# The up projection of a ConvFFN on fp16 halves, with a scale measured by squares in the mLSTM, and the next unit's first products inside a unit

## The chip, the cores and the metric

The kernel runs on one core of one Trainium2 chip. The metric is device time in microseconds (us), the median of several runs. The engines are PE (matrix), DVE (vector), ACT (scalar functions), POOL and SP; each works through a queue of its own in order, and a DMA is started by a row in one of these queues. PEld is PE's loading of weights.

## The reference

One layer of a diffusion backbone: 1024 latent tokens of width 1024, and 256 context tokens. Both are normalised, modulated and projected; windowed attention and a bidirectional chunkwise mLSTM (4 heads, chunks of 128, so 2 context and 8 latent chunks in each direction) work side by side; the branches are gated and merged, and a ConvFFN with 2816 hidden channels follows. What the change touches is the FFN's up projection, and the mLSTM beside which its scale is now measured:

```python
def conv_ffn(h, w_up, conv_w, conv_b, w_down):      # h (1,1024,1024), w_up (1024, 5632)
    u = h @ w_up
    up = jnp.pad(u, ((0, 0), (1, 1), (0, 0)))
    acc = conv_b
    for j in range(3):
        acc = acc + up[:, j:j + L] * conv_w[j]
    a, g = jnp.split(acc, 2, axis=-1)
    return (jax.nn.silu(g) * a) @ w_down

# in the layer
ht, ht_c = mlstm_bidirectional(...)                 # scans over chunks, state C, n, m
ml = mlstm_readout(ht, mo, ml_norm_w[l])            # rms_norm(h) * norm_w * sigmoid(mo)
y = merge_branches(att, ml, ga, gm, w_branch_att[l], w_branch_ml[l], w_out[l])
x_mid = x + g1[:, None, :] * y
x = x_mid + g2[:, None, :] * conv_ffn(modulate(rms_norm(x_mid, norm2_w[l]), sh2, sc2), w_up[l], ...)
```

## The kernel before

Products that need more than one half-precision pass are made of pairs: an operand is split into a high part and a low part, and high x high, high x low and low x high are summed in PSUM (the three matmul lines 163 to 165 and, in `product`, 2027 to 2029). `split_from` makes a pair: ACT copies to the high part (L47), DVE subtracts it from the source for the low part, with one tensor_tensor (L54) where there is no scale and one scalar_tensor_tensor (L56) where a scale is given. The combined input projection has fp16 pairs with a scale measured from the weights; the up projection and the branch products have fp32r pairs without a scale.

The up projection runs in 22 units (`NFC`, 128 hidden channels and their 128 gates each). A unit multiplies 1024 x 256 weight columns by the 1024 tokens with seven products in place of eight (a Winograd scheme of 2 x 2 blocks): two first products with `b11` and `b21` on the raw left columns (`r1`), then `t2`, `t1` (on `q1`), `t3`, `b22` (on `q2`) and `t4` (on `r2`). Each is 4 blocks of 3 matmuls 128x128 by 128x512. `Units.lead` loads a unit's weights (1 MB) and splits `r1`; `prep` and `prep2` form the sums `s` on DVE and split `q1`, `q2` and `r2`. `rest` runs the five later products; PSUM banks `pa` and `pb` are used two and three times in a unit and are emptied to the outputs `ua` and `ug` between. Behind a unit, `conv_gate` applies the width-3 convolution, the SiLU and the gate (L2165 to L2171), and `weight_sums` and `hidden_sums` make sums for the down projection (L1906, L2182 to L2185). After the units the down projection follows (`dx`, L2027 again), and there `last_row` (L2306, L2308) forms the second half of a modulation vector row by row on DVE.

In the mLSTM each head has `proj_kv` (k and v for 8 latent chunks, L47 copies k and VH out of PSUM), `proj_q`, `masked`, `states`, `core` (the recurrence: state C on DVE, its high part CH on ACT, outputs nm out of PSUM on ACT, L1487), `proj_o` (output gate mo), `readout` (squares of the result hf on ACT, a power on POOL, L1520 and L1521, and the scaling of hf on DVE, L1524) and `turn` (transposes mt on PE, L1532, and the gated product mo on DVE, L1534). The next head's projections are written between; after the last head the branch products follow (yb, with operands baa and baw).

The order of the work on each engine is set by the framework's scheduler, by its own estimates of when work is ready, and not by the order in which the program is written; tiles come from pools with a fixed number of buffers, and a new tile waits until an old one's readers are done.

Of the kernel before, what the change touches and what calls it, by code (L numbers as in the profile page):

```python
# [18 lines left out]
P = 128  # L19
# [153 lines left out]
def layer_kernel(ctx: ExitStack, tc: tile.TileContext, A: dict, out: bass.AP, dbg=None):  # L173
# [69 lines left out]
    E.hs = cp.tile([P, 2], F32, name="hs")  # L243
    E.w2 = ScaledWeights(E, tc, ph1)
# [1017 lines left out]
def stage_mlstm(E, st):  # L1262
# [84 lines left out]
    def proj_q(h):  # L1347
# [4 lines left out]
        for t in range(2):  # L1352
# [3 lines left out]
            split_from(nc, qh, ql, ps, scale=f[:, 4:5])  # L1356
            qT.append((qh, ql))
# [16 lines left out]
    def proj_o(h):  # L1374
        w = H[h]["wqo"]
        sgs = [rp.tile([P, 2, 512], F32, tag="sg", name=f"sg{h}_{t}", bufs=2) for t in range(2)]
        for t in halves(h):
            for v in range(2):
# [3 lines left out]
                nc.scalar.activation(sgs[t][:, v], ps, fn, scale=H[h]["fqo"][:, 4:5])  # L1382
        H[h]["sg"] = sgs
# [182 lines left out]

    rwp = st.enter_context(tc.tile_pool(name="mlr4", bufs=4, reuse_waits="tile"))
# [7 lines left out]
    E.kvx.close()  # L1575
    trans_k(0)
# [3 lines left out]
    for _ in range(2):  # L1580
        branch_sums()
    for h in range(MLH):
# [14 lines left out]
        if h + 1 < MLH:  # L1597
            proj_q(h + 1)
            for _ in range((3, 4, 3)[h]):
                branch_sums()  # L1600


def stage_tail(E, st):
# [51 lines left out]


# [179 lines left out]
    def norm_factors():  # L1836

        nc.vector.scalar_tensor_tensor(m2[:, 1], m2[:, 1], 1.0, vecT[:, V_N2 : V_N2 + KT], op0=ALU.add, op1=ALU.mult)
        nc.vector.tensor_scalar(m2[:, 1], m2[:, 1], float(D) ** 0.5, None, op0=ALU.mult)

# [43 lines left out]
    def put(m, k, src, s=slice(0, 512)):  # L1884
        if B.setdefault(m, [None] * H)[k] is None:
            B[m][k] = [x512(f"{m}{x}{k}", pool=homes[m]) for x in "hl"]
# [50 lines left out]
    def weight_sums(k, a0, a1, b0, b1, eng=None):  # L1937
# [11 lines left out]
        nc, lambda j: A["w_up"][j], lambda n: rawp.tile([P, KT, 256], F32, tag="raw", name=n), op4, op2,  # L1949
# [14 lines left out]
    norm_factors()  # L1964
# [19 lines left out]
    U.prep_apart(0, lambda n, dt=F32R: x512(n, dt, 1))  # L1984
# [47 lines left out]
class Units:  # L2032
# [3 lines left out]
    def __init__(self, nc, src, raw, op4, op2, bank, out, B):  # L2036
        self.nc, self.src, self.raw, self.op4, self.op2, self.bank, self.out, self.B = nc, src, raw, op4, op2, bank, out, B
# [10 lines left out]
    def pair(self, j, nm, new, src):  # L2048
        p = self.v(new(f"{nm}h{j}")), self.v(new(f"{nm}l{j}"))
        split_from(self.nc, *p, src)  # L2050
        return [(p[0][:, k], p[1][:, k]) for k in range(p[0].shape[1])]

    def lead(self, j):
        self.raws[j] = raw = self.raw(f"ur{j}")
        self.nc.sync.dma_start(raw, self.src(j))
        if j != 2:
            self.R1[j] = self.pair(j, "r1", self.op4, raw[:, :, 0:P])

    def lead_first(self, j):
# [3 lines left out]
        self.R1[j] = self.pair(j, "r1", self.op4, raw)  # L2063
# [20 lines left out]
    def prep(self, j):  # L2084
# [6 lines left out]
        self.Q[j] = [self.pair(j, "q1", self.op4, s12)]  # L2091

    def prep2(self, j):
# [5 lines left out]
        self.Q[j] += [self.pair(j, "q2", self.op4, s34), self.pair(j, "r2", self.op2, a22)]  # L2099

    def prep_apart(self, j, new):
# [3 lines left out]
        s1, s2, s3, s4 = [self.v(new(f"s{i}_{j}", F32)) for i in range(1, 5)]  # L2105
# [4 lines left out]
        self.Q[j] = [sum([self.pair(j, f"q1{i}", new, s) for i, s in enumerate((s1, s2))], [])]  # L2110
        self.S[j] = s3, s4

    def prep2_apart(self, j):
        h, lo = [self.v(self.op4(f"q2{x}{j}")) for x in "hl"]
        for i, s in enumerate(self.S.pop(j)):
            split_from(self.nc, h[:, 4 * i : 4 * i + 4], lo[:, 4 * i : 4 * i + 4], s)
        r2 = self.pair(j, "r2", self.op2, self.raws.pop(j)[:, 4:8, P:256])
        self.Q[j] += [[(h[:, k], lo[:, k]) for k in range(8)], r2]

    def rest(self, j):  # L2120
        nc, B, op = self.nc, self.B, self.op
        pa, ua = self.mid.pop(j)
        if j not in self.Q:
            self.prep(j)
        if len(self.Q[j]) == 1:
            self.prep2(j)
# [17 lines left out]
def stage_ffn(E, st):  # L2144
# [94 lines left out]
    a = None  # L2239
    for j in range(NFC):  # L2240
        if j > 2:
# [207 lines left out]
```

## Time and profile before

| | us |
|---|---|
| median of 3 runs (1845.82 to 1847.97) | 1846.55 |
| the profiled execution | 1849.14 |
| its span | 1847.4 |
| PE busy | 1790.8 (97%) |
| DVE busy | 1425.9 (77%) |
| ACT busy | 1069.8 (58%) |
| POOL busy | 508.3 (28%) |
| mean granted TensorE clock | 0.988 of full speed |

The span starts with the projection and attention; the mLSTM's own work lies at about 600 to 955, the branch products and the merge to about 1200, the up projection from there to about 1640, and the down projection to the end. Rows of the profile read: line, engine, operation, output <- input, and count; then busy time and mean time of one, and idle time of the engine before it with what ended it. A time at a row's start is from the span's start.

### The profile page before, as it was taken

What the parts mean: (1) busy time and instruction counts of PE and PEld (TensorE: products, weight loads), DVE (VectorE), ACT (ScalarE), POOL (GpSimd) and SP (SyncE); (2) the same over time, 40 slices, a digit from 0 to 9 for tenths busy, and PEclk for the clock granted to TensorE, in tenths of its full rate; (3) what the DMA queues carried; (4) which work ended last, traced back from release to release, by engine and by line L of the source; (5) the groups of instructions that cost most, each with busy time, mean ns of one, the idle gap of its engine ahead of it and who ended that gap; (6) DMA issues with size and microseconds to landing.
All of it is one profiled execution on the core that took longest, in us unless ns stands there. A gap on an engine that the chain in (4) does not pass through costs nothing.

```text
span 1847.4 us, 27864 instructions
## 1 busy us (share of the span) xinstructions
PE 1790.8 (97%) x9207; PEld 1283.5 (69%) x9207; DVE 1425.9 (77%) x2864; ACT 1069.8 (58%) x2229; POOL 508.3 (28%) x747
## 2 busy tenths in 40 slices
PE   7989999999998899999999999999999999999999
PEld 3855555555554566656668887878888888888887
DVE  3858888888788686858687787698889898897665
ACT  4747877878787565645356462476444444465441
POOL 2467769587862530303010020000000000000000
PEclk9999999999999899999999999999999999999999
DMA  9747988888796625261359927322454544599751
GB/s 342 233 138 146 201 170 179 192 180 199 147 182 131 219 79 192 79 213 37 132 188 368 344 92 246 141 77 106 172 207 180 194 160 166 195 318 371 260 172 69
DMA packets 302193, 342.47 MB, mean 185 GB/s; under 512 B 176208, under 2 KB 200672, under 8 KB 299232
## 3 DMA queue, kind: packets, MB, share of 16 engines
q1 hardware_dynamic: 287648, 314.47, 56.3%
q10 hardware_dynamic: 14400, 26.22, 4.2%
q8 instruction: 72, 1.18, 0.3%
q14 instruction: 73, 0.60, 0.1%
HBM read 224.61 MB, written 76.16 MB: 163 GB/s over the span
## 4 chain that ended last, share of the span: by engine, by line
PE 78%; DVE 7%; DMA 4%; issue 3%; ACT 3%; POOL 3%; SPq 0%; ACTq 0%; DVEq 0%; POOLq 0%
PE g L706 8%; PE pq L706 6%; PE pa L2027 4%; PE pa L2029 4%; PE pa L2028 4%; PE po L706 3%; PE dx L2029 2%; PE dx L2027 2%; PE dx L2028 2%; PE pb L2027 2%; PE pb L2029 2%; PE pb L2028 2%; PE yb L2029 2%; PE yb L2027 2%; PE yb L2028 2%
## 5 line engine op out<-in xcount | busy, mean ns | idle before, releaser
L850 DVE CUSTOM_DVE_ANT_0 s<-s,maskA,nsink 128x640 f32<-128x640 f32 (+1 forms) x128 | 117.4, 917 | 65.5 <-PE s L845 65.0
L866 DVE TENSOR_TENSOR P<-s,P 128x640 f16<-128x640 f32 (+1 forms) x128 | 100.6, 786 | 1.0 <-ACT s L861 1.0
L860 ACT ACTIVATE P<-s,st 128x640 f16<-128x640 f32 (+1 forms) x128 | 98.2, 767 | 4.1
L706 PE MATMUL g<-hH,fh 128*128 128x512 f16 x256 | 97.1, 379 | 0.0
L706 PE MATMUL g<-hH,fl 128*128 128x512 f16 x256 | 97.0, 379 | 0.0
L706 PE MATMUL g<-hL,fh 128*128 128x512 f16 x256 | 97.0, 379 | 0.0
L861 ACT ACTIVATE s<-s,st 128x640 f32<-128x640 f32 (+1 forms) x128 | 93.8, 733 | 0.0
L706 PEld LDWEIGHTS <-hH 128*128 128x128 f16 x640 | 62.8, 99 | 37.3 <-issue 1.8
L858 ACT ACTIVATE st<-st,shift 128x1 f32<-128x1 f32 x128 | 37.6, 294 | 85.6 <-DVE st L850 84.8
L706 PE MATMUL pq<-wha,hH 128*128 128x384 f16 (+1 forms) x256 | 84.9, 332 | 0.1
L706 PE MATMUL pq<-wha,hL 128*128 128x384 f16 (+1 forms) x256 | 84.9, 332 | 0.0
L706 PE MATMUL pq<-wla,hH 128*128 128x384 f16 (+1 forms) x256 | 84.9, 332 | 0.0
L706 PEld LDWEIGHTS <-fh 128*128 128x128 f16 x512 | 49.2, 100 | 45.4
L2165 ACT ACTIVATE cv<-ua,vecT 128x1024 f32<-128x1024 f32 x22 | 27.4, 1246 | 84.9 <-DVE ua L2138 84.9
L1436 POOL TENSOR_SCALAR kwh<-k,gcall 128x128 fp32r<-128x128 f32 x72 | 32.5, 455 | 157.2 <-PE dC L164 53.9
L47 ACT ACTIVATE dfh<-drf 128x512 fp32r<-128x512 f32 x55 | 34.4, 628 | 59.3 <-PE dx L2028 26.5
L2027 PE MATMUL dx<-dwh,dfh 128*128 128x512 f32 (+1 forms) x176 | 68.3, 388 | 0.0
L2029 PE MATMUL dx<-dwh,dfl 128*128 128x512 f32 (+1 forms) x176 | 68.2, 388 | 0.0
L2028 PE MATMUL dx<-dwl,dfh 128*128 128x512 f32 (+1 forms) x176 | 68.2, 387 | 0.0
L54 DVE TENSOR_TENSOR dfl<-drf,dfh 128x512 fp32r<-128x512 f32 x55 | 37.6, 688 | 36.1 <-ACT dfh L47 36.1
L165 PE MATMUL kv<-whkv,hL 128*128 128x384 f16 x192 | 62.6, 326 | 0.0
L164 PE MATMUL kv<-wlkv,hH 128*128 128x384 f16 x192 | 62.6, 326 | 0.0
(691 smaller groups left out, 6249.9 us busy)
## 6 DMA issues: line engine op xcount, KB each, us to landing
ur<-in_w_up SPq DMA_DIRECT2D x22, 1024.0 KB
wmb<-in_w_modB SPq DMA_DIRECT2D x48, 256.0 KB
f_d<-cv SPq DMA_DIRECT2D x22, 512.0 KB
wm<-in_w_modA SPq DMA_DIRECT2D x16, 512.0 KB
fr<-in_w_g SPq DMA_DIRECT2D x32, 256.0 KB
drf<-fs_d SPq DMA_DIRECT2D x15, 512.0 KB
drw<-wt_d SPq DMA_DIRECT2D x14, 512.0 KB
w1b<-in_w_cx SPq DMA_DIRECT2D x16, 388.0 KB
```

The lines of the kernel that those rows point to most:

```text
L54: rest = nc.vector.tensor_tensor(lo, src, whole, op=ALU.subtract)
L164: nc.tensor.matmul(ps, lh[:, ls], rl[:, rs], start=False, stop=False)
L165: nc.tensor.matmul(ps, ll[:, ls], rh[:, rs], start=False, stop=stop and i == n - 1)
L706: nc.tensor.matmul(self.ps, x, w, start=self.i == 0, stop=self.i == self.n - 1)
L850: nc.vector.tensor_tensor_reduce(e, e, self.mask, scale=self.ss[:, h : h + 1], scalar=nsink[:, hh : hh + 1], op0=ALU.add, op1=ALU.min, acc ...
L858: nc.scalar.activation(m, st4[:, 8 + h : 9 + h], AF.Identity, bias=shift)
L860: nc.scalar.activation(two[:, :W], e, AF.Exp, bias=m, scale=-1.0)
L861: nc.scalar.activation(e, e, AF.Exp, bias=m, scale=-1.0, accum_out=st4[:, 4 + h : 5 + h])
L866: nc.vector.tensor_tensor(two[:, W : 2 * W], self.e[h], two[:, :W], op=ALU.subtract)
L2027: nc.tensor.matmul(ps, lh, rh, start=start and i == 0, stop=False, skip_group_check=True)
L2028: nc.tensor.matmul(ps, lh, rl, start=False, stop=False, skip_group_check=True)
L2029: nc.tensor.matmul(ps, ll, rh, start=False, stop=stop and i == n - 1, skip_group_check=True)
```

## The change

Three things are changed.

1. The up projection's operands are fp16 pairs. The two halves of a pair share one tile, so a pair takes half the bytes. The weights' splits are given a scale, `E.upf[:, 2:3]`, and so use L56 in place of L54; the token operands (`b11`, `t1` and so on) are split without one.
2. The scale is measured: the up weights (23 MB) are loaded once more in 44 pieces of 512 KB from ACT's queue, 3 buffers in all, and squared with a running sum by 44 ACT instructions of 128x1024. These are written into heads 1 to 3's `proj_kv` and `proj_q` and heads 0 to 2's `proj_o`. `up_scales`, behind the last head's `proj_o`, sums them over partitions with a ones-matmul and makes the factors on DVE and POOL; it also scales the modulation `m2` and the convolution's columns.
3. In a unit from the third on, the next unit's two first products stand inside: t2, t1, next b11, t3, b22, next b21, t4. The next unit's `prep` and `prep2` are written between these, and `lead` two units ahead.

```diff
+    def up_load():
+        n = UP["load"]
+        if n < NUP:
+            raw = UP["raw"][n] = upp.tile([P, 4, 256], F32, tag="up", name=f"um{n}")
+            nc.scalar.dma_start(raw, A["w_up"][n // 2][:, 4 * (n % 2) : 4 * (n % 2) + 4])
+            UP["load"] += 1
+    def up_square(k):
+        for _ in range(k):
+            ...
+                nc.scalar.activation(raw, raw, AF.Square, accum_out=E.up[:, n : n + 1])
+                UP["done"] += 1
+                up_load()
+    def up_scales():
+        f, g, m2, vecT = E.upf, E.upf[:, 8:], E.m2[:, 1:3], E.vecT
+        ...
+        nc.tensor.matmul(pb[:, : NUP + 2], E.ones, E.up[:, : NUP + 2], start=True, stop=True)
+        nc.vector.tensor_reduce(f[:, 0:1], pb[:, :NUP], axis=AX.X, op=ALU.add)
+        nc.vector.tensor_scalar(g[:, 2:4], pb[:, NUP : NUP + 2], 1.0, 1e-30, op0=ALU.mult, op1=ALU.add)
+        nc.gpsimd.tensor_scalar(f[:, 1:2], f[:, 0:1], 2.0 ** -28, 1e-36, op0=ALU.mult, op1=ALU.add)
+        nc.gpsimd.tensor_tensor(f[:, 2:3], f[:, 1:2], expo[:, 0:1], op=ALU.pow)
+        ...
+        nc.gpsimd.tensor_tensor(f[:, 3:4], g[:, 4:5], expo[:, 0:1], op=ALU.pow)
+        nc.vector.reciprocal(f[:, 4:6], f[:, 2:4])
+        nc.gpsimd.tensor_tensor(f[:, 6:7], f[:, 4:5], f[:, 5:6], op=ALU.mult)
+        nc.gpsimd.tensor_scalar(m2, m2, f[:, 3:4], None, op0=ALU.mult)
+        cw = vecT[:, V_CW : V_CW + 132]
+        nc.gpsimd.tensor_scalar(cw, cw, f[:, 6:7], None, op0=ALU.mult)
...
 proj_kv, for h > 0 and each latent chunk:
+            if h and j >= NCB:
+                up_square(1)
 proj_q, for h > 0 and each half:
+                up_square(2 if h == MLH - 1 else 1)
 proj_o, each product:
+                if h < MLH - 1:
+                    up_square(1)
+        if h == MLH - 1:
+            up_scales()
...
     def pair(self, j, nm, new, src):
-        p = self.v(new(f"{nm}h{j}")), self.v(new(f"{nm}l{j}"))
-        split_from(self.nc, *p, src)
+        p = [self.v(t) for t in new(f"{nm}{j}")]
+        split_from(self.nc, *p, src, scale=self.scale)
...
     def rest(self, j, new=None, between=lambda i: None):
         ...
         product(nc, pb, op(q1, 0), B["t1"], True)
         copy_act(nc, ug[:, t1], pb)
+        between(0)
+        if new is not None:
+            r1 = self.R1.pop(new)
+            na, un = self.bank("A", f"pa{new}"), self.out("u", f"ua{new}")
+            product(nc, na, self.op(r1, 0), B["b11"], True)
+            copy_act(nc, un[:, t0], na)
         product(nc, pa, op(q2, 0), B["t3"], False)
         nc.vector.tensor_tensor(ug[:, t1], pa, ug[:, t1], op=ALU.add)
+        between(1)
         product(nc, pb, op(q2, 4), B["b22"], False)
         nc.vector.tensor_tensor(ua[:, t1], pb, ua[:, t1], op=ALU.add)
+        if new is not None:
+            pc = self.bank("C", f"pc{new}")
+            product(nc, pc, self.op(r1, 4), B["b21"], True)
+            nc.vector.tensor_tensor(un[:, t0], pc, un[:, t0], op=ALU.add)
+            self.mid[new] = na, un
         product(nc, pa, op(r2, 0), B["t4"], False)
```

At the end of the mLSTM, DVE's queue held the two groups of hf one behind the other (the number at a name's end tells tiles apart, `rr_0` and `rr_1` are the two halves' factors):

```order
L1524 TENSOR_SCALAR hf_11521<-hf_11521,rr_0_12050 128x256 x4
L1524 TENSOR_SCALAR hf_11521<-hf_11521,rr_1_12065 128x256 x4
L1534 SCALAR_TENSOR_TENSOR mo_0_0_12085<-mt_0_0_12080,mlw,sg_0_11944 128x512
L1534 SCALAR_TENSOR_TENSOR mo_0_1_12093<-mt_0_1_12088,mlw,sg_0_11944 128x512
L54 TENSOR_TENSOR bawl_0_12182<-bawr_12179,bawh_0_12181 128x512
L54 TENSOR_TENSOR baal_0_12228<-baar_12225,baah_0_12227 128x512
L54 TENSOR_TENSOR bawl_1_12184<-bawr_12179,bawh_1_12183 128x512
```

Now, in the same place of DVE's queue:

```order
L1533 TENSOR_SCALAR hf_11658<-hf_11658,rr_0_12207 128x256 x4
L1606 TENSOR_REDUCE upf<-upq 128x1
L1607 TENSOR_SCALAR upf<-upq 128x2
L1533 TENSOR_SCALAR hf_11658<-hf_11658,rr_1_12222 128x256 x2
L1615 RECIPROCAL upf<-upf 128x2
L1533 TENSOR_SCALAR hf_11658<-hf_11658,rr_1_12222 128x256 x2
L1543 SCALAR_TENSOR_TENSOR mo_0_0_12242<-mt_0_0_12237,mlw,sg_0_12081 128x512
L1543 SCALAR_TENSOR_TENSOR mo_0_1_12250<-mt_0_1_12245,mlw,sg_0_12081 128x512
```

The reduction, which reads the ones-matmul's result `upq`, stands between the groups, and the reciprocal between the halves of the second. On POOL, at the same place, the two halves' factors were followed by nothing of the mLSTM; now the queue reads (with what each waits for):

```order
L1529 TENSOR_SCALAR rr_1_12222<-rr_1_12222 128x4 [waits Activation_49]
L1608 TENSOR_SCALAR upf<-upf 128x1 [waits DVE_49]
L1530 TENSOR_TENSOR rr_1_12222<-rr_1_12222,expo 128x4 [waits Pool_49]
L1609 TENSOR_TENSOR upf<-upf,expo 128x1 [waits Pool_49]
L1610 TENSOR_TENSOR upf<-upf,expo 128x1 [waits DVE_49]
L1611 TENSOR_TENSOR upf<-upf 128x1 [waits Pool_49]
L1612 TENSOR_SCALAR upf<-upf 128x1 [waits Pool_49]
L1613 TENSOR_SCALAR upf<-upf 128x1 [waits Pool_49]
L1614 TENSOR_TENSOR upf<-upf,expo 128x1 [waits Pool_49]
```

The second half's power (L1530) stands behind a step that waits for DVE's reduction. Inside the mLSTM, ACT's queue in the second head's `proj_kv` held, before, copies of k and VH and squares of the next head's weights (wjw):

```order
L47 ACTIVATE k_8_8638<-kv_8_8639,wfw_ml_8492 128x128
L47 ACTIVATE VH_8_8665<-kv_8_8639,wfw_ml_8492 128x256
L1550 DMA s_ba_1_9024<-in_w_ba 128x512 x2
L112 ACTIVATE wjw_ml_1_9684,wqw_ml_9681<-wrw_ml_1_9675 128x768
L112 ACTIVATE wjw_ml_2_9686,wqw_ml_9681<-wrw_ml_2_9677 128x768
```

Now, between copies of the same kind, it holds squares of the up weights (um) and the loads of later pieces:

```order
L47 ACTIVATE k_8_8664<-kv_8_8665,wfw_ml_8515 128x128
L47 ACTIVATE VH_8_8691<-kv_8_8665,wfw_ml_8515 128x256
L1592 ACTIVATE um_8698,upq<-um_8698 128x1024
L1592 ACTIVATE um_8734,upq<-um_8734 128x1024
L1584 DMA um_8822<-in_w_up 128x1024
L47 ACTIVATE k_7_8700<-kv_7_8701,wfw_ml_8515 128x128
L47 ACTIVATE VH_7_8727<-kv_7_8701,wfw_ml_8515 128x256
```

The squares of the next head's weights stand later in the queue. In the up projection, DVE's queue held, before, from the next unit's sum with `pc` to its next sum (units 9 to 11):

```order
L1906 TENSOR_TENSOR wb_16066<-wb_16066 128x512
L2167 SCALAR_TENSOR_TENSOR cv_31_16083<-ug_15975,vecT,cv_31_16083 128x1023
L2077 TENSOR_TENSOR ua_16116<-pc_16091,ua_16116 128x512
L54 TENSOR_TENSOR q1l_16196<-s_11_16192,q1h_16195 128x1024
L2171 TENSOR_TENSOR cv_9_16079<-cv_9_16079,cv_31_16083 128x1024
L2097 TENSOR_TENSOR s_11_16199<-ur_16186 128x512
L2098 TENSOR_TENSOR s_11_16199<-ur_16186,s_11_16192 128x512
L54 TENSOR_TENSOR r2l_16207<-ur_16186,r2h_16206 128x512
L54 TENSOR_TENSOR q2l_16203<-s_11_16199,q2h_16202 128x1024
L54 TENSOR_TENSOR r1l_16334<-ur_16331,r1h_16333 128x1024
L2136 TENSOR_TENSOR ug_16120<-pa_16090,ug_16120 128x512
```

Now (from unit 12's last sum, with the preparations of units 15 to 17):

```order
L2208 TENSOR_TENSOR ua_16383<-pb_16489,ua_16383 128x512
L2259 TENSOR_TENSOR fa_16605<-fa_16605 128x512
L2164 TENSOR_TENSOR s_15_16823<-ur_16736 128x512
L2260 TENSOR_TENSOR fs_16606<-cv_11_16478,fa_16605 128x512
L2241 SCALAR_TENSOR_TENSOR cv_12_16614<-ua_16383,vecT,cv_12_16614 128x1023
L2212 TENSOR_TENSOR ua_16524<-pc_16573,ua_16524 128x512
L2242 SCALAR_TENSOR_TENSOR cv_12_16614<-ua_16383,vecT,cv_12_16614 128x1023
L2165 TENSOR_TENSOR s_15_16823<-ur_16736,s_15_16789 128x512
L56 SCALAR_TENSOR_TENSOR r_16965<-ur_16872,upf,r_16965 128x512
L2241 SCALAR_TENSOR_TENSOR cv_34_16618<-ug_16490,vecT,cv_34_16618 128x1023
L56 SCALAR_TENSOR_TENSOR q_16826<-s_15_16823,upf,q_16826 128x1024
L2242 SCALAR_TENSOR_TENSOR cv_34_16618<-ug_16490,vecT,cv_34_16618 128x1023
```

The next unit's sum with its second first product (`pc`) comes right behind the unit's own last sum, the splits are L56, and the preparations run up to three units ahead of the products, where they ran one to two ahead. The eight rows of `last_row` for the first piece (`u<-w_modB`) stood behind all units and now stand among the sums of units 2 to 8.

More of the change, by code (lines that the diff above doesn't have):

```diff
@@ L1581, in stage_mlstm @@
         branch_sums()
+    for _ in range(3):
+        up_load()
     for h in range(MLH):
@@ L1600, in stage_mlstm @@
                 branch_sums()
+    ux.close()
 def stage_tail(E, st):
@@ L2032, with __init__ @@
 class Units:
-    def __init__(self, nc, src, raw, op4, op2, bank, out, B):
-        self.nc, self.src, self.raw, self.op4, self.op2, self.bank, self.out, self.B = nc, src, raw, op4, op2, bank, out, B
+    def __init__(self, nc, src, raw, op4, pair4, pair2, scale, bank, out, B):
+        self.nc, self.src, self.raw, self.op4, self.pair4, self.pair2, self.bank, self.out, self.B = nc, src, raw, op4, pair4, pair2, bank, out, B
+        self.scale = scale
         self.raws, self.R1, self.mid, self.S, self.Q = {}, {}, {}, {}, {}
```

92 lines of the change are left out of this document (60 added, 32 removed).

## The prediction

> **What bounds the kernel now.** I read the page's busy times and chain first, to see which engine can be the limit; then the windows by stage, since the average mixes stages; then the matmuls of two stages one by one, for the price of each type.
>
> ```profile
> PE 1790.8 (97%) x9207; PEld 1283.5 (69%) x9207; DVE 1425.9 (77%) x2864; ACT 1069.8 (58%) x2229; POOL 508.3 (28%) x747
> PE 78%; DVE 7%; DMA 4%; issue 3%; ACT 3%; POOL 3%; SPq 0%; ACTq 0%; DVEq 0%; POOLq 0%
> ```
>
> PE is busy for 97% of the span and is 78% of the chain. What takes time from PE shortens the kernel; what leaves PE without work lengthens it.
>
> ```profile
> 640.00:750.00 110.00, 108.44 (x656) 73.22 (x655) 84.17 (x255) 64.78 (x151) 28.24 (x79) 0.99 0.37 122
> 750.00:850.00 100.00, 94.90 (x567) 62.54 (x567) 72.17 (x208) 54.79 (x128) 22.87 (x63) 0.98 0.42 139
> 850.00:950.00 100.00, 99.24 (x596) 64.62 (x595) 73.09 (x220) 52.30 (x126) 17.28 (x39) 1.00 0.31 105
> 1200.00:1250.00 50.00, 48.38 (x226) 39.20 (x225) 46.30 (x99) 34.81 (x75) 3.02 (x2) 1.00 0.22 74
> 1300.00:1400.00 100.00, 100.00 (x442) 82.79 (x442) 87.99 (x104) 47.90 (x58) 0.00 (x0) 1.00 0.53 198
> 1500.00:1600.00 100.00, 100.00 (x443) 82.81 (x442) 89.15 (x107) 47.76 (x59) 0.00 (x0) 1.00 0.45 169
> ```
>
> After the window and its length the columns are PE, PEld, DVE, ACT and POOL busy, granted clock, DMA share and GB/s. From 1300 to 1600, the up projection, PE is busy without a gap at clock 1.00, with DVE behind it at 88 to 89%. From 640 to 950, the mLSTM, PE lacks 7.4 us of 310 (110 - 108.44 + 100 - 94.90 + 100 - 99.24), and ACT is busy for 171.9 us (64.78 + 54.79 + 52.30). At 1200 to 1250, the way into the up projection, DVE has 46.30 of 50 us and PE lacks 1.6.
>
> **The change, part by part.**
>
> *The pitch of the products.* The first two rows below are the same product of two units in turn in the up projection, the last two the same kind of matmul 21 places apart in the mLSTM, on fp16 operands.
>
> ```profile
> 1403.64 0.39 PE L2027 MATMUL pa<-b11h,r1h 128*128 128x512 f32 x1
> 1422.68 0.39 PE L2027 MATMUL pa<-b11h,r1h 128*128 128x512 f32 x1
> 945.04 0.38 PE L165 MATMUL mo<-hH,wlqo 128*128 128x512 f16 x1
> 949.57 0.38 PE L165 MATMUL mo<-hH,wlqo 128*128 128x512 f16 x1
> ```
>
> A unit has 7 products of 4 blocks of 3 matmuls, 84 in all: 19.04 / 84 = 0.2267 us from one start to the next. The fp16 ones have 4.53 / 21 = 0.2157. The change keeps the count and shape, so 22 x 84 = 1848 matmuls lose 0.0110 each: **-20.3 us**, or 18.12 us a unit for 19.04. The load of weights shrinks too:
>
> ```profile
> L2027 PEld LDWEIGHTS pa<-t3h,q2h 128*128 128x128 f32 x64 | 12.0, 188 | 2.5
> L165 PEld LDWEIGHTS <-wlqo 128*128 128x128 f16 x16 | 1.6, 98 | 1.9
> ```
>
> At 188 ns under a pitch of 227 it was hidden in the main; that it leaves 11 ns is seen only in the pitches. [...]
>
> *The splits.* A split is an ACT copy to the high half and a DVE subtraction for the low half. With the scale, DVE's plain subtraction becomes a three-operand one:
>
> ```profile
> L54 DVE TENSOR_TENSOR q2l<-s,q2h 128x1024 fp32r<-128x1024 f32 x16 | 19.6, 1226 | 14.7 <-ACT q2h L47 14.7
> L54 DVE TENSOR_TENSOR r2l<-ur,r2h 128x512 fp32r<-128x512 f32 x17 | 11.6, 683 | 0.0
> L2088 DVE TENSOR_TENSOR s<-ur 128x512 f32<-128x512 f32 x16 | 11.1, 692 | 16.4 <-PE pb L2028 16.1
> L2166 DVE SCALAR_TENSOR_TENSOR cv<-ua,vecT,cv 128x1023 f32<-128x1023 f32 x16 | 20.5, 1280 | 0.8
> L56 DVE SCALAR_TENSOR_TENSOR ql<-q,wfw_mlqo,qh x6: 744/750/751, 723.6 to 913.2; 128x512 fp32r<-128x512 f32 x6
> L2308 DVE SCALAR_TENSOR_TENSOR u<-u,sil,u x14: 741/746/752, 1645.1 to 1684.4; 128x512 f32<-128x512 f32 x14
> ```
>
> 1280 for 1226 and 750 for 683: 0.054 us on each of three splits and 0.067 on one, 0.23 us a unit. DVE had 16.8 us a unit (88% of 19.04) and gets 17.0 of 18.12, so PE stays the bound. Moving the next unit's preparations ahead of the last three products, with buffers of half the size, takes DVE's 16.1 us of waits for PE away. One thing speaks against: the order puts eight rows of the second modulation vector (L2308, 0.746 us), which stood in the down stage, into units 2 to 8. With DVE's row lengths above, units 3 to 8 then hold 18.7, 19.3, 18.7, 19.2, 18.7 and 18.0 us of DVE work. The five above 18.12 overrun by 4.0 us together. Two products (24 matmuls, 5.2 us) now stand between a sum and the product that needs its bank, so part hides: bounds 0 and 4, taken **+1.5 us**, nearer to hidden.
>
> At the way in, DVE (46.30 of 50) and not PE sets the pace, so the fp16 gain of the first products is lost there, and scaled splits are longer: ACT's copy with a scale takes 688 ns for 620.
>
> ```profile
> L47 ACT ACTIVATE qh<-q,wfw_mlqo 128x512 fp32r<-128x512 f32 x6 | 4.1, 688 | 25.0 <-PE q L165 19.9 <-DMA s_bm<-in_w_bm 5.1
> L47 ACT ACTIVATE r2h<-ur 128x512 fp32r<-128x512 f32 x16 | 9.9, 620 | 0.0
> ```
>
> Two units' first products (2 x 24 x 0.011 = 0.5 us) and some eight splits of 0.07 make **+1.0 us**, bounds 0.3 and 1.5.
>
> *The squares in the mLSTM.* 44 loads of 512 KB and 44 squares are added on ACT. A square's nearest row is the sigmoid of its shape, and its sum is read out as here:
>
> ```profile
> L1515 ACT ACTIVATE sg<-sg 128x1024 f32<-128x1024 f32 x6 | 6.3, 1050 | 0.0
> L112 ACT ACTIVATION_READ_ACCUMULATOR wjw_mlqo<-wrw_mlqo 128x1 f32 x10 | 1.9, 190 | 0.0
> L1487 ACT ACTIVATE nm<-i,gcall 128x257 f32<-128x257 f32 x64 | 30.2, 474 | 42.6 <-PE i L165 30.0 <-POOL hf L1494 6.3 <-DVE nm L1491 1.7
> L47 ACT ACTIVATE CH<-C 128x258 fp32r<-128x258 f32 x62 | 24.8, 415 | 7.8 <-DVE C L1444 7.5
> PE o L163 <- ACT sh L47: 1.5, 1, 1.5
> PE S L163 <- DVE ql L56: 1.5, 3, 0.9
> PE kT L1365 <- ACT k L47: 1.0, 1, 1.0
> ```
>
> 44 x 1.24 = 54.6 us: ACT's 171.9 of 310 become 226.5, 73%. There is room, and ACT waits for others anyway (30.0 us for PE ahead of nm). But a square stands in ACT's queue ahead of the k, VH, CH and nm copies, which PE's next matmuls need, and holds them up to 1.24 us; a late load holds the queue too, and the loads raise the traffic from a mean of 122 GB/s by 23 MB / 310 us = 74, to what the up projection has at a DMA share of 0.53. Lower bound: the work fits in gaps and the shifted order takes some of PE's waits away, -2. Upper bound: of the 30 chunk steps in the three heads with squares (10 each) every one loses a third of a square, +12. If PE's 7.4 us of waits grow as ACT's work does (by 226.5 / 171.9), it is 2.4. A load now stands in ACT's queue ahead of the first head's copies, for which I add 1. **+3.5 us**.
>
> *The end of the mLSTM.* Here the scales are made, between the last head's output gate and its readout.
>
> ```profile
> 949.96 1.14 DVE L1524 TENSOR_SCALAR hf<-hf,rr 128x256 f32<-128x256 f32 x4 [2.78 <-POOL rr L1521]
> 951.53 1.14 DVE L1524 TENSOR_SCALAR hf<-hf,rr 128x256 f32<-128x256 f32 x4 [0.43 <-POOL rr L1521]
> 955.60 1.41 DVE L1534 SCALAR_TENSOR_TENSOR mo<-mt,mlw,sg 128x512 f32<-128x512 f32 x2 [2.93 <-PE mt L1532]
> 954.75 0.38 PE L165 MATMUL mo<-hH,wlqo 128*128 128x512 f16 x1
> 954.97 2.10 PE L1532 MATMUL mt<-ident,hf 128*128 128x128 f32 x16
> 959.54 0.50 PE L2027 MATMUL yb<-baah,bawh 128*128 128x512 f32 x1 [2.48 <-ACT bawh L47]
> 959.88 0.40 PE L2028 MATMUL yb<-baal,bawh 128*128 128x512 f32 x1
> 962.60 0.96 PE L2029 MATMUL yb<-baah,bawl 128*128 128x512 f32 x3 [0.47 <-DVE bawl L54]
> 950.21 0.19 POOL L1520 TENSOR_SCALAR rr<-rr 128x4 f32<-128x4 f32 x1 [0.28 <-ACT rj L1519]
> 950.49 1.01 POOL L1521 TENSOR_TENSOR rr<-rr,expo 128x4 f32<-128x4 f32 x1
> L122 POOL TENSOR_TENSOR wfw_ml<-wfw_ml,expo x3: 547/547/547, 680.6 to 866.1; 128x1 f32<-128x1 f32 x3
> ```
>
> Before, all hf were scaled by 952.7, and the 16 transposes followed the last mo without a gap. Now DVE's reduction for the scale stands between the two groups of hf and waits for a ones-matmul that PE's queue has behind its last mo (954.75). POOL's second power of rr stands behind the step that waits for this reduction; the last two hf stand behind a reciprocal that waits for three more powers of one column (0.547 each) and three small steps (0.19 each). So: matmul done 955.2, reduction 955.5, POOL's step and the four-column power (1.01) to 956.9, then 1.6 of powers, 0.6 of small steps and 0.4 between them (0.08 each, as from 950.21 + 0.19 to 950.49) to 959.5, reciprocal and two hf to 960.4, where the first mo can start on DVE. Before, 7.0 us lay from the first mo (955.60) to the yb products with bawl (962.60), with the same work on DVE between; so these come at 967.4, **+4.8 us**. PE's clock comes on top: at 959.54 the yb matmuls start 0.34 us apart, where the up projection's have 0.2267, so a longer gap adds slow time: +0.6, for **+5.4 us**; bounds 2 (part of the tail's splits move into the gap) and 7. [...]
>
> The conv columns' scaling and the moved modulation steps are small POOL and DVE work far from their readers: nothing.
>
> **Sum.** -20.3 + 1.5 + 1.0 + 3.5 + 5.4 = -8.9 us. The profiled execution took 1849.14 us (span 1847.4), 2.6 above the median of 1846.55, so it becomes 1840.2, and the median **1837.6 us**.
>
> **The rivals.**
>
> *Nearly the full gain.* The squares fit into ACT's gaps and the end is absorbed, as ACT's 45% of free time speaks for: -20.3 + 1.0 + 1 = -18.3, **1828 us**.
>
> *Slower: squares hold the recurrence.* ACT is in order and busy for 55% of the time; if that part of the squares stands ahead of a copy that PE needs at once, the body costs 0.55 x 54.6 = 30 us and not 3.5: 1846.55 - 12.4 + 30 = **1864 us**. It is slower by over 0.2% from a body of 16.1 us on. PE's waits for ACT there, 1.5 and 1.0 us, speak against it; the in-order queue speaks for it. Between 8.7 and 16.1 it is no change.
>
> [...]
>
> *The pitch doesn't change*, if something other than the type sets it: then only the costs of 11.4 are left, **1858 us**; the mo rows speak against it.
>
> **How the numbers follow.** Forecast (1831 to 1843) 0.54; nearly full gain 0.21; a body of 8.7 to 16.1 us, 0.13; held recurrence 0.08; DVE bound 0.02; no shorter pitch 0.02. 0.2%, 3.7 us, is about what measurement tells from no change: faster 0.75, same 0.13, slower 0.12. The low bounds of all terms together give 1827 (-20.3 + 0 + 0.3 - 2 + 2 = -20); the high ones 1851; the range 1826 to 1848 leaves out the ends of the last cases.
>
> **What would show it.** In the changed kernel's trace: 18.1 us from one b11 product to that of the next unit, DVE near 94% there with no PE wait past unit 8; PE waits on DVE in units 3 to 8 of up to 4 us; 44 squares of about 1.05 us with PE's waits from 640 to 950 grown by few us; and hf, mt and bawl in line after POOL's powers, the yb products late by 4 to 5. A pitch of over 0.22, ACT waiting for its loads, or PE idle of 20 us in the mLSTM would make it wrong.

## The result, and the profile after

The changed kernel took 1879.91 us (median of 4 runs, 1878.95 to 1882.38), the kernel before 1846.67 beside it. The ratio is 1.0181, 95% interval 1.0164 to 1.0199: slower by 33 us, where 9 us faster was forecast.

The page of the changed kernel, busy times and shares of the chain:

```profile
PE 1789.9 (95%) x9209; PEld 1130.0 (60%) x9209; DVE 1430.6 (76%) x2867; ACT 1120.3 (60%) x2321; POOL 517.0 (28%) x758
PE 64%; DVE 17%; DMA 8%; POOL 4%; issue 3%; ACT 2%; SPq 0%; ACTq 0%; DVEq 0%; POOLq 0%
```

PE fell from 78% of the chain to 64%; DVE went from 7 to 17 and DMA from 4 to 8. The span grew by 29.8 us (1847.4 to 1877.2). I split it at the same instructions in both traces: first and last mo product, first yb product, first product of the up projection, first product of the down projection.

| stretch | before | after | difference |
|---|---|---|---|
| start to first mo product | 640.6 | 635.0 | -5.6 |
| first to last mo product (the mLSTM's four heads) | 314.2 | 354.0 | +39.8 |
| last mo to first yb product | 4.8 | 14.8 | +10.0 |
| first yb product to the up projection | 249.0 | 249.7 | +0.7 |
| up projection | 423.6 | 408.1 | -15.5 |
| down projection to the end | 215.3 | 215.7 | +0.4 |

The first row can't be read as the change's: the kernels of the experiments below, whose code up to there differs at most in the first loads of pieces, start their first mo anywhere from 634.7 to 638.9, and of before there is one profile. The other rows have a spread too: runs of one and the same mLSTM code took 313.6, 314.6 and 316.3 us there (e8, e12 and e11), and the up projection with the changed kernel's units 407.9 to 410.6. The two windows of the mLSTM, before and then after, from first to last mo product (columns as in the prediction: window and length, then PE, PEld, DVE, ACT and POOL busy, granted clock, DMA share and GB/s):

```profile
640.60:954.75 314.15, 306.74 (x1834) 202.03 (x1834) 231.07 (x687) 171.95 (x405) 69.60 (x183) 0.99 0.37 124
635.00:989.00 354.00, 324.93 (x1840) 214.62 (x1840) 230.81 (x679) 216.47 (x496) 71.90 (x180) 0.93 0.52 170
```

PE's idle time grew from 7.4 to 29.1 us, and its busy time for nearly the same matmuls by 18.2, at a granted clock of 0.93 for 0.99. So half of the 40 us is waiting, and the other half slower matmuls around the waits: from 695 to 715 us PE has no wait and the clock is 1.00, in the next two stretches of 20 us it waits for 2.7 and 5.9 us at 0.83 and 0.87. ACT's busy time grew by 44.5 us, where 54.6 had been counted: the read of a square's sum overlaps the rows beside it (two squares start at 721.40 and 722.44, the read between them at 722.35), so that a square takes some 1.04 us and not 1.24.

Where the waits come from is seen in two views of the changed kernel. First the chain that ended last, between 716 and 751 us (start, length, piece):

```profile
716.72 6.28 DMA s_ba<-in_w_ba
723.08 0.70 DVE s_ba L1560
...
731.34 3.15 DMA s_ba<-in_w_ba
...
737.75 8.85 DMA s_ba_d<-s_ba
747.07 0.44 ACTq L1567
747.55 2.75 DMA t_at<-attT_d
750.31 0.67 DVE t_at L1568
```

Then ACT's timeline and PE's in the same place; ACTq rows are DMAs issued from ACT's queue, and the bracket gives the idle time before a row and what ended it:

```profile
729.83 1.97 ACTq L1559 DMA_DIRECT2D s_ba<-in_w_ba  x4
731.84 0.63 ACT L47 ACTIVATE sh<-ub 128x512 fp32r<-128x512 f32 x1 [8.27 <-issue]
746.69 1.79 ACTq L1567 DMA_DIRECT2D t_at<-attT_d  x4
748.53 0.73 ACT L47 ACTIVATE CH<-C 128x258 fp32r<-128x258 f32 x2 [9.24 <-issue]
749.67 0.58 PE L163 MATMUL o<-VH,sh 128*128 128x258 f32 x1 [4.45 <-ACT nm L1496]
```

These are the branch sums (`branch_sums` in the code): 12 rounds spread over the heads that prepare operands for the branch products. A round loads four 256 KB blocks from ACT's queue into two buffers, DVE forms four sums, SP stores them, and the next round needs the same two buffers. In the changed kernel's chain one store took 8.85 us, so ACT's queue stood for 9.24 us at the next round's load, and the copies CH and nm, for which PE then waits, stood behind it in ACT's queue. In the chain of the kernel before, the stores of this kind in the mLSTM were these:

```profile
803.61 2.00 DMA t_at_d<-t_at
814.84 3.15 DMA t_at_d<-t_at
```

DVE waits for the loads as well, since its sums stand in its queue among the recurrence's work. Its waits for the first two kinds of sums (us in all, times, longest), first two rows in the changed kernel and last two in the kernel before:

```profile
DVE t_at L1568 <- DMA t_at<-attT_d: 16.9, 4, 6.2
DVE s_ba L1560 <- DMA s_ba<-in_w_ba: 6.4, 2, 5.9
DVE t_at L1560 <- DMA t_at<-attT_d: 4.6, 3, 1.9
DVE s_ba L1551 <- DMA s_ba<-in_w_ba: 1.2, 2, 0.7
```

The third kind, s_bm, had 4.0 us after and 5.0 before.

The end of the mLSTM, PE, DVE, SP and ACT of the changed kernel in turn:

```profile
992.61 0.51 PE L1541 MATMUL mt<-ident,hf 128*128 128x128 f32 x2 [1.19 <-DVE hf L1533]
995.24 0.75 PE L1541 MATMUL mt<-ident,hf 128*128 128x128 f32 x2 [2.12 <-DVE hf L1533]
1003.72 0.79 PE L2093 MATMUL yb<-baah,bawh 128*128 128x512 f32 x1 [6.44 <-ACT bawh L47]
1004.31 0.63 PE L2094 MATMUL yb<-baal,bawh 128*128 128x512 f32 x1
994.77 0.17 DVE L1615 RECIPROCAL upf<-upf 128x2 f32<-128x2 f32 x1 [2.04 <-POOL upf L1614]
995.38 1.39 DVE L1543 SCALAR_TENSOR_TENSOR mo<-mt,mlw,sg 128x512 f32<-128x512 f32 x2
996.14 0.99 SPq L1544 DMA_DIRECT2D mlT_d<-mo  x2
997.22 0.40 SPq L1801 DMA_DIRECT2D bawr<-in_w_ba  x1
1003.04 1.15 ACT L47 ACTIVATE bawh<-bawr 128x512 fp32r<-128x512 f32 x2 [9.74 <-DMA bawr<-in_w_ba]
```

The forecast chain is there: the reciprocal waits for POOL's power, and the first mo on DVE comes 6.4 us after the last mo product (989.0), where it came 0.85 after it before. Behind it is a step the forecast did not have. SP's queue holds the store of that mo (996.14) ahead of a load of branch weights, bawr (997.22), which lands at 1003.0; ACT waits 9.74 us for it and PE 6.44. In the kernel before, the last of these in_w_ba loads was issued ahead of the stores:

```profile
946.04 0.65 SPq L1729 DMA_DIRECT2D bawr<-in_w_ba  x1
956.38 0.98 SPq L1535 DMA_DIRECT2D mlT_d<-mo  x2
```

The up projection, two units' first rows in the changed kernel (PE), a wait of PE in an earlier unit, and the splits on DVE and ACT from 1300 to 1600:

```profile
1545.16 0.38 PE L2093 MATMUL pa<-b,r 128*128 128x512 f16 x1
1563.29 0.38 PE L2093 MATMUL pa<-b,r 128*128 128x512 f16 x1
1426.73 0.38 PE L2093 MATMUL pa<-t,r 128*128 128x512 f16 x1 [1.16 <-DVE ug L2205]
L56 DVE SCALAR_TENSOR_TENSOR q<-s,upf,q 128x1024 f16<-128x1024 f32 x37 | 47.4, 1281 | 7.5 <-ACT q L47 7.3
L2246 DVE TENSOR_TENSOR cv<-cv,cv 128x1024 f32<-128x1024 f32 x16 | 19.6, 1223 | 0.1
L47 ACT ACTIVATE q<-s,upf 128x1024 f16<-128x1024 f32 x36 | 41.3, 1147 | 48.6 <-DVE s L2165 26.5 <-DVE s L2156 22.1
```

The first and the late units take 18.13 us (1563.29 - 1545.16), as forecast (18.12); eight units in the middle take 18.2 to 19.45, together 3.9 us over the pace. PE's rows with idle time there, 2.3 us in all, wait for DVE's sums.

### The profile page after: what moved, and what is told of

Same layout as the page of the kernel before. It is cut to its first block, busy times and chain, and to the rows that moved or that the text cites. A ratio compares the mean times of both kernels' runs of the same rounds, so it can differ in the third digit from the quotient of the medians.

```text
span 1877.2 us, 27971 instructions
## 1 busy us (share of the span) xinstructions
PE 1789.9 (95%) x9209; PEld 1130.0 (60%) x9209; DVE 1430.6 (76%) x2867; ACT 1120.3 (60%) x2321; POOL 517.0 (28%) x758
## 4 chain that ended last, share of the span: by engine, by line
PE 64%; DVE 17%; DMA 8%; POOL 4%; issue 3%; ACT 2%; SPq 0%; ACTq 0%; DVEq 0%; POOLq 0%
PE g L707 7%; PE pq L707 5%; PE po L707 3%; PE yb L2093 2%; PE yb L2095 2%; PE yb L2094 2%; PE dx L2095 2%; PE dx L2093 2%; PE dx L2094 2%; PE kv L164 2%; PE kv L165 2%; PE kv L163 2%; PE dy L2095 2%; PE dy L2094 2%; PE dy L2093 2%
## 5 line engine op out<-in xcount | busy, mean ns | idle before, releaser
L47 ACT ACTIVATE q<-s,upf 128x1024 f16<-128x1024 f32 (+1 forms) x46 | 50.8, 1108 | 60.0 <-DVE s L2165 30.3
L54 DVE TENSOR_TENSOR dfl<-drf,dfh 128x512 fp32r<-128x512 f32 x55 | 37.8, 690 | 49.0 <-ACT dfh L47 48.9
L2093 PE MATMUL pa<-t,q 128*128 128x512 f16 x176 | 66.7, 379 | 0.9 <-ACT ua L47 0.9
L2094 PE MATMUL pa<-t,q 128*128 128x512 f16 x176 | 66.7, 379 | 0.0
```

Source lines behind the costliest of these rows:

```text
L47: return nc.scalar.activation(out, in_, AF.Copy, scale=scale)
L54: rest = nc.vector.tensor_tensor(lo, src, whole, op=ALU.subtract)
L2093: nc.tensor.matmul(ps, lh, rh, start=start and i == 0, stop=False, skip_group_check=True)
L2094: nc.tensor.matmul(ps, lh, rl, start=False, stop=False, skip_group_check=True)
```

## The experiments

What had to be told apart was the 40 us of the mLSTM: ACT's time for the squares, the loads, the branch sums between them, or an order that changed for another reason. In these tables and texts "the mLSTM" runs from first to last mo product, and the gap from there to the first yb product. The kernel before, run beside them, had medians of 1844.4 to 1845.7 us.

**Without measuring (e1) and with the scales made early (e2).** e1 leaves out loads and squares and sets the sums to 1.0; e2 also moves `up_scales` ahead of the mLSTM.

```diff
     E.up = mp.tile([P, 64], F32, name="upq")
+    nc.gpsimd.memset(E.up, 1.0)
-        if n < NUP:          # in up_load and up_square
+        if n < MEAS:         # MEAS = 0
```

> The 44 loads and 44 squares of the up weights are left out; the sums they would fill are set to 1.0 (the expected value), and all else of the change stays, the making of the scales behind the last output gate too. The changed kernel takes 354 us from the first head's first mo product to the last head's last one, the kernel before 314 (640.6 to 954.8). If the measuring (loads and squares together) is what lengthens the mLSTM: 312 to 318 us there, the up projection at 408 as in the changed kernel, the end of the mLSTM still some 5 us late; in all 1833 to 1840 us. If the mLSTM is long for another reason (buffers taken from it, an order that changed with the other edits): still over 340 us there and over 1865 in all.

> As the run without loads and squares, with the making of the scales moved ahead of the mLSTM, so that neither the ones-matmul nor POOL's powers stand between the last output gate and the readout. If the last head's readout pays for the scales' chain and for the loads of the branch operands behind it in SP's queue: the first yb product comes 5 us after the last mo (4.8 before, 14.7 in the changed kernel), and the kernel is 5 us faster than with the scales at the end, 1828 to 1834 us. If the scales cost nothing there by themselves (the gap of 14.7 us comes of loads that are late in any case): no difference between the two, within 2 us.

e1: 1833.22 us, ratio 0.9934 (0.9919 to 0.9948); mLSTM 313.8, gap 4.8, up projection 410.6. e2: 1831.31 us, 0.9926 (0.9907 to 0.9946); mLSTM 313.6, gap 4.8. The measuring is what lengthens the mLSTM, and all the rest of the change together is worth 12 us. The guesses on the gap missed: it was 4.8 with the scales at the end too, and e2 was 1.9 us faster than e1 and not 5, for in e1's order the reduction stands behind both groups of hf on DVE, and the loads of bawr ahead of the stores on SP.

**Squares without loads (e3), loads without squares (e4).** e3 squares one resident piece 44 times; e4 loads all pieces and squares 8 columns of each.

```diff
e3:
-                nc.scalar.activation(raw, raw, AF.Square, accum_out=E.up[:, n : n + 1])
+                nc.scalar.activation(UP["keep"][1 + n % 2], UP["keep"][0], AF.Square, accum_out=E.up[:, n : n + 1])
e4:
+                nc.scalar.activation(raw[:, 0, 0:8], raw[:, 0, 0:8], AF.Square, accum_out=E.up[:, n : n + 1])
```

> All 44 squares stay on ACT, but they read one piece that is loaded once; the other 43 loads are left out. If ACT's time is the cost (a square stands ahead of the copies that PE needs): most of the 40 us stays, over 340 us in the mLSTM and 1865 to 1880 in all. If the loads are the cost (traffic, and branch sums that DVE must wait for): the mLSTM takes 314 to 325 us and the kernel 1835 to 1850.

> All 44 loads stay, but each square reads 8 columns in place of 1024 (about 0.2 us and the read of the sum in place of 1.24). If the loads are the cost: over 340 us in the mLSTM and 1860 to 1880 in all, with DVE waiting for the loads of the branch sums (t_at, s_ba) as in the changed kernel, 24 us for 11 before. If ACT's time is the cost: 314 to 325 us in the mLSTM and 1835 to 1850 in all.

e3: 1833.03 us, 0.9937 (0.9912 to 0.9963). e4: 1843.92 us, 0.9993 (0.9979 to 1.0007), mLSTM 326.0. The window of e3's mLSTM:

```profile
637.40:948.50 311.10, 302.99 (x1833) 201.02 (x1832) 229.97 (x685) 214.41 (x495) 70.81 (x182) 1.00 0.37 125
```

ACT has the same 214 to 216 us of work as in the changed kernel, and PE idles 8.1 us: the squares alone cost nothing. The loads alone cost 12 us in the mLSTM, just above the 314 to 325 us that were expected if ACT's time was the cost; both together cost 40, so neither theory held alone, and something between them had to be found.

**The branch sums' loads on SP's queue (e5).**

```diff
-                nc.scalar.dma_start(o, src)          # s_ba, s_bm; likewise t_at
+                nc.sync.dma_start(o, src)
```

> The full change, with the loads of the branch sums (s_ba, t_at, s_bm) issued from SP's queue in place of ACT's; the 44 loads and squares of the up weights stay where they were. Measured so far: squares alone cost nothing (1833.0 us), loads alone 10.7 (1843.9 for 1833.2 without either), both 46.7 (1879.9). Theory A: a branch sum's two buffers are free only when the sums before it are stored; the added loads make these stores slow (8.9 us in the chain), ACT's queue stands at the next sums' load (8.3, 9.2 and 7.6 us in the changed kernel), and the copies that PE needs stand behind. Then with the loads on SP, ACT has no wait of over 4 us at a branch sum, the mLSTM takes 315 to 330 us for 354, and the kernel 1835 to 1855. Theory B, the traffic itself: loads and stores are as slow as before, DVE waits for them in its own queue, and the kernel stays over 1865.

1857.38 us, 1.0064 (1.0039 to 1.0089); mLSTM 339.5, gap 4.8. DVE's waits in the mLSTM of this run:

```profile
DVE s_bm L1560 <- DMA s_bm<-in_w_bm: 20.2, 3, 7.6
DVE t_at L1568 <- DMA t_at<-attT_d: 15.0, 3, 5.6
DVE s_ba L1560 <- DMA s_ba<-in_w_ba: 8.3, 1, 8.3
```

Between the two theories: ACT no longer stands at the issue of a branch sum, the mLSTM is 14.5 us shorter, but the sums are late all the same and DVE now waits 54 us for their loads (with a second t_at row of 10.3). Where the load is issued decides which queue stands, and with SP's it costs less: 1857.4 us for 1879.9, of which 10.0 are the gap at the end.

**Half and a quarter of the pieces (e6, e8), and the scales ahead of the last recurrence (e7, e8).**

```diff
e6 (STEP = 2), e8 (STEP = 4):
-            if n < NUP:
+            UP["calls"] += 1
+            if n < NUP and UP["calls"] % STEP == 0:
...
-                UP["done"] += 1
+                UP["done"] += STEP
...
+        nc.gpsimd.tensor_scalar(f[:, 1:2], f[:, 0:1], STEP * 2.0 ** -28, 1e-36, op0=ALU.mult, op1=ALU.add)
e7, e8:
     for h in range(MLH):
+        if h == 3:
+            up_scales()
         core(h)
```

> Every second piece of the up weights is loaded and squared (22 of 44, 11.5 MB), and the sum is doubled; all else as in the change. If the cost grows with the traffic: half of the 46.7 us over the kernel without measuring is left, 1853 to 1860. If it comes of a queue that stands only when the loads fill the gaps between branch sums (theory A, with a threshold): well under half, 1833 to 1845.

> The full change, with the making of the scales written ahead of the last head's recurrence, where all 44 squares are done, and not behind its output gate. In the changed kernel 14.7 us lie between the last mo product and the first yb product, 4.8 in the kernel before. If the scales' chain through POOL makes this gap: it goes back to 5, and the kernel to about 1870. If the rest of it is the branch weights' load (bawr), which stands behind the stores of mo in SP's queue in this order too: the gap is 9 to 11, for the first mo on DVE comes 5.6 us earlier and the load as much, and the kernel is at 1874.

> Every fourth piece is loaded and squared (11 of 44, 5.8 MB), the sum is multiplied by four, and the scales are made ahead of the last head's recurrence. By theory A and by traffic alike little of the 46.7 us is left: 1831 to 1840 us, 314 to 318 in the mLSTM, a gap of 5 at its end. Slower than 1845 would say that the number of loads is not what matters.

e6: 1836.29 us, 0.9957 (0.9941 to 0.9974), mLSTM 315.5: half of the pieces cost 3 us and not 23. e8: **1830.19 us, 0.9923 (0.9908 to 0.9938)**, mLSTM 313.6, gap 4.8, up projection 409.3; it beats both kernels, with a scale that is estimated from a quarter of the weights. The scales' early place counts for little there: e1, with its scales at the end, has the same gap of 4.8.

e7: 1878.95 us, 1.0182 (1.0163 to 1.0202); gap 11.3 for 14.8. Its rows, PE's and SP's:

```profile
993.26 1.14 PE L1539 MATMUL mt<-ident,hf 128*128 128x128 f32 x8 [0.83 <-DVE hf L1531]
1001.28 0.80 PE L2093 MATMUL yb<-baah,bawh 128*128 128x512 f32 x1 [6.88 <-ACT bawh L47]
992.88 2.04 SPq L1542 DMA_DIRECT2D mlT_d<-mo  x2
995.02 0.38 SPq L1801 DMA_DIRECT2D bawr<-in_w_ba  x1
```

No transpose waits for a power of the scale any more, yet the load of bawr still stands behind the stores of mo, and PE waits 6.9 us for it. Of the 10 us at the end, 3.5 go with the scales' chain. The other 6.5 go with the place of that load, which no run moved by itself; the kernel as a whole came out 1 us faster, where 1874 was expected.

**Without branch sums (e9), and with two buffers (e10).** e9 measures in full and neither loads nor computes branch sums; the same bytes are stored from a constant tile. e10 has `bufs=2` in the pool of the pieces.

```diff
e9, branch_sums:
-        two = [rp.tile([P, 4, DV], F32, tag="sg", ...) for j in range(2)]
-        ... loads and sums
+        for j in range(4):
+            for o in (0, 256):
+                nc.sync.dma_start(E.sums_d[n][:, j, i, o : o + 256], zz)
```

> The full change with all 44 loads and squares, but the branch sums (s_ba, t_at, s_bm) are neither loaded nor computed in the mLSTM; the same bytes are stored from a constant tile, so the branch products run on these. With the branch sums' loads on SP the kernel went from 1879.9 to 1857.4 us, with ACT's waits moved to DVE (58 us of waits for these loads). If the loads of the up weights cost only because each branch sum (load, four sums on DVE, store, the next load in the same two buffers) becomes slow and ACT, DVE or SP stands at it: the mLSTM takes 305 to 316 us with the full measuring, and the kernel 1825 to 1838. If loads and squares together burden the recurrence itself: still over 335 us there.

> The full change with two buffers of the up weights' pieces in place of three, so that at most two loads are in flight; all 44 loads and squares stay. If the rate of the loads is what slows the branch sums: the mLSTM takes 325 to 345 us for 354, and the kernel 1850 to 1868. If the number of loads decides and not how many fly at once: 350 us or more, as ACT now also waits for the pieces, and 1875 to 1890.

e9: 1831.63 us, 0.9935 (0.9918 to 0.9951). Its mLSTM:

```profile
637.00:949.00 312.00, 302.49 (x1839) 201.05 (x1839) 205.66 (x646) 216.68 (x502) 73.23 (x182) 1.00 0.50 159
```

All 44 loads and squares are in it, with DMA engines as busy as in the changed kernel (0.50 for 0.52), and PE idles 9.5 us at full clock. The measuring costs only where branch sums stand in its way. Which part of a round it is, e9 can't say: with the sums go their loads and 25 us of DVE's work (205.66 for 230.81). A third buffer for the rounds was not tried, so how much hangs on the two buffers is not shown. e10: 1875.93 us, 1.0162 (1.0135 to 1.0189), mLSTM 351.1: fewer loads in flight do not help; ACT then waits for the pieces too (8.5 us).

**The place and the number (e13, e14).** e13 writes 32 of the squares into the recurrences (`core`) in place of `proj_kv` and `proj_q`; e14 takes 33 of 44 pieces in the old places.

```diff
e13:
                     output(d, i, order[i], order[i] not in seen)
                     seen.add(order[i])
+                up_square(1)
```

> All 44 loads and squares and all branch sums stay; 32 of the squares (and so the loads behind them) are written into the recurrences of the four heads, one for each latent chunk, in place of proj_kv and proj_q, where the branch sums stand too; the 12 in proj_o stay. If the bunching with the branch sums makes the cost: the mLSTM takes 314 to 326 us and the kernel 1830 to 1846. If the volume makes it (44 loads and 12 branch sums do not fit one beside the other wherever they stand): 340 us or more, and over 1860.

> 33 of the 44 pieces, three of every four in their places, all else as in the change; mLSTM so far: 314 us without pieces and with 11, 315.5 with 22, 354 with 44. If the cost starts where the pieces fill the time between branch sums and grows from there (volume): 330 to 340 us, the kernel at 1850 to 1862. If it is one unlucky order that only the full number gives: 315 to 322 us, 1835 to 1842.

e13: 1852.87 us, 1.0032 (1.0020 to 1.0044), mLSTM 335.0. e14: 1847.66 us, 1.0006 (0.9995 to 1.0017), mLSTM 324.4. Neither guess was right for e13, which fell between, and e14 lies between its two guesses. In one table:

| loads, squares | branch sums | mLSTM, us | kernel, us |
|---|---|---|---|
| 0, 0 (e1) | yes | 313.8 | 1833.2 |
| 11, 11 (e8) | yes | 313.6 | 1830.2 |
| 22, 22 (e6) | yes | 315.5 | 1836.3 |
| 33, 33 (e14) | yes | 324.4 | 1847.7 |
| 44, 44, of which 32 in the recurrences (e13) | yes | 335.0 | 1852.9 |
| 44, 44 in the projections (the change) | yes | 354.0 | 1879.9 |
| 44, 8 columns each (e4) | yes | 326.0 | 1843.9 |
| 1, 44 (e3) | yes | 311.1 | 1833.0 |
| 44, 44 (e9) | no | 312.0 | 1831.6 |

Up to 22 pieces cost next to nothing, 33 cost 11 us in the mLSTM and 44 cost 21 or 40, depending on their place. How much of that is traffic in the instant and how much the order that the scheduler makes of each variant was not separated: each variant gets an order of its own, and e4 against the change shows that the squares matter once the loads are there.

**The unit order (e11) and the eight rows (e12),** both on e8. e11 has the units' order of the kernel before with fp16 halves; e12 pins the rows of `last_row` behind the last unit on DVE.

```diff
e11:
+        if j > 2:
+            U.first_mm(j)
+        if j > 1:
+            U.first_ev(j)
+        u = U.rest(j)
e12, last_row:
+        with tc.issue_after(E.gated.ins):     # the last unit's gate on DVE
             if k == 0:
```

> A quarter of the pieces (as in the run at 1830.2 us, up projection 409.3 us), and the units in the order of the kernel before: first products of a unit, then t2, t1, t3, b22, t4, with the next unit loaded and prepared behind; fp16 halves as in the change. If fp16 alone makes the gain and the moved first products are worth nothing: 406 to 411 us there, the kernel at 1828 to 1832. If the moved products are needed since DVE has 17.0 of 18.1 us and PE would wait at the end of a product for its bank: 412 to 425 us, 1833 to 1846.

> A quarter of the pieces, with the eight rows of the modulation vector that stand among units 2 to 8 on DVE pinned behind the last unit, where the kernel before has them. In the changed kernel units 7 to 15 take 18.2 to 19.45 us for 18.13. If these rows are what makes DVE late: 18.13 in every unit, the up projection 405 to 406 us for 409.3, the kernel at 1826 to 1828. If the rows were filler and DVE is late by itself: 409, no change.

e11: 1843.21 us, 0.9987 (0.9976 to 0.9998), up projection 420.2 for 409.3. PE's largest waits there:

```profile
PE pa L2096 <- ACT ua L47: 9.3, 11, 2.9
PE pa L2096 <- DVE ug L2208: 1.4, 3, 0.9
```

fp16 alone, in the old order, is worth 3.4 us of the 423.6; the new order (the moved first products, and the earlier preparations with them) makes the other 11. In the old order the bank `pa` is used again behind one other product, and PE waits 11 times, 9.3 us in all, for ACT's copy out of it. That this copy stands behind splits that wait for DVE is an estimate from the changed kernel, where ACT stands 48.6 us for DVE's sums ahead of its q<-s,upf rows; no row of e11 here shows it. e12: 1829.78 us, 0.9921 (0.9906 to 0.9936), up projection 408.0: seven units still take 18.4 to 19.3 us. The kernel is 0.4 us faster than e8, and the up projection 1.3 us shorter, which is less than the spread of the runs with the same units (407.9 to 410.6). The units run 3.9 us over the pace of 18.13, as in the changed kernel, where the rows stand among them, and 5.0 over it in e8. So the rows are not shown to make DVE late; what does was not found.

## Why the prediction was wrong, point by point

- *The pitch*: right. -20.3 us was worked out, units take 18.13 us where nothing waits. 18.13 / 84 is 0.2158 us from one start to the next, for the 0.2157 read from the fp16 rows of the kernel before.
- *The splits*: mechanism right, size at the upper bound. 1281 ns on DVE was forecast from 1280; the units lost 3.9 us for 1.5, bounds 0 and 4. The eight rows, the reason given, are not shown to be it: without them the units lost 3.9 us too (e12). So it is luck that the size lies within the bounds. The way in is what is left, 0.9 for 1.0 (423.6 became 408.1: -15.5 = -20.3 + 3.9 + 0.9), closer than the spread of 2.7 us allows to be read. That DVE becomes the bound, a chance of 0.02, did not come: the changed kernel's scaled splits took 1281 ns beside a plain 1223 (cv<-cv,cv), its other three-operand rows on two fp32 tensors 1277 (cv<-ug,vecT,cv), and the products of the up projection waited 2.7 us for DVE in all (2.3 for sums, 0.4 for a split).
- *The squares in the mLSTM*: the step that failed. +3.5 us was taken, bounds -2 and 12; it was 40. The term priced ACT's time in the queue, which by itself costs nothing (e3). The loads were dismissed by mean traffic, 196 GB/s, which was nearly right (170) and not the point: the branch sums, a serial round of load, sums, store and load through two buffers, stood in a row that the prediction itself quoted (ACT's qh waited 5.1 us for s_bm), and were not priced. Nor was the slow clock around the waits (0.93 for 0.99), half of the loss. The prediction's own sign of being wrong, PE idle of 20 us in the mLSTM, came with 29.1.
- *The rival of held copies* had the place, ACT's queue ahead of the copies, and the size nearly right by luck (30 for 40 us), but the wrong holder: not the squares, which it priced, but loads that wait for a buffer.
- *The end of the mLSTM*: +5.4 taken, bounds 2 and 7. Of these 4.8 were for the gap, which grew by 10.0, and 0.6 for a slow clock behind it, where the next stretch grew by 0.7. The chain through POOL came as worked out: first mo on DVE 5.6 us later for 4.8. The other part is a queue that was not looked at: SP's, where a load moved behind the stores (e7). In e5 and e6 the scales are made at the end too, but the order has the load ahead of the stores and the reduction behind both groups of hf: the gap is 4.8. The 0.6 was right by luck: it was read from yb rows 0.34 us apart at 959.54, behind a wait of 2.48 us, but the clock granted in the kernel before was 1.00 from 957.1 to 968, so these rows do not show the term. In the changed kernel it was 0.50 in that place (1003.7 to 1009).
- *Nothing for the rest* (convolution columns, modulation): right, as far as e1 shows it: all that is left is 12 us faster. That this meets the forecast without squares, -12.4, is luck in its parts: in e1 the gap at the end did not grow, where 4.8 were forecast, and the up projection gained 13.0 (423.6 to 410.6) of 17.8.

## What to carry to other kernels

Before work is put into an engine's free time, look in its queue for instructions that wait for a buffer or a transfer: in the mLSTM here ACT's longest stand at such a load was 9.24 us with the work that was added, for 5.1 before, and the copies that stood behind it paid. Mean utilisation said nothing here on a serial round of load, compute, store and reload in the same buffers; price such a round by its slowest transfer (8.85 us for a store here, where the mean traffic was 170 GB/s), and count a slow clock behind PE's longer waits (0.50 behind 6.44 us here). A measured scale need not read everything: a quarter of the loads cost no time that could be seen (1830.2 us, and 1831.3 without any), though no run tries it on other weights.

## What the runs showed of the hardware

- After PE's 6.44 us without work the yb matmuls started 0.43 us apart (1004.31 to 1008.58, 11 matmuls) at a granted clock of 0.50 before they returned to 0.23, twice the pitch for some 5 us. A wait of 2.48 us in the same place of the kernel before left the clock at 1.00 (957.1 to 968), and its longest yb matmul took 501 ns; in e1, with a wait of 2.3 us there, the longest took 793, as in the changed kernel (792). From which wait on the clock falls is not shown.
- A copy on ACT to fp16 with a scale from memory took 714 ns for 626 without at 128x512 (r<-ur,upf and b<-acc of the changed kernel).
